# Mixture of experts streamed through one core: branch arms of 64 and 32 slots replaced by blocks of 32 slots with short conditionals

## The chip, the cores and the metric

One core of a Trainium2 chip runs the whole program. The metric is device time in microseconds for one execution, given as the median of several runs.

## The reference

The program computes one layer of a streaming encoder over 256 tokens of width 1024: a normalised input goes through three branches (sparse attention, a convolution, attention into a memory), which are gated, summed and projected; after a layer norm comes a mixture of experts, which is where the change lies. Each token takes its 4 best of 32 experts:

```python
logits = (xt @ w_router + b_router)
top_v, top_e = lax.top_k(logits, 4)
gate = softmax(top_v)
# for each expert e, over the tokens that chose it:
hdn = xb @ w1[e] + b1[e]                 # 1024 -> 2048
g, u = split(hdn, 2)
g = minimum(g, 7.0); u = clip(u, -7.0, 7.0)
y = ((u + 1.0) * (g * sigmoid(1.702 * g))) @ w2[e] + b2[e]   # 1024 -> 1024
out = segment_sum(y * gate, token)
h = layer_norm(alpha * h + out)
```

No token is dropped, so an expert has as many rows as tokens chose it. With these inputs the counts, from e0 to e31, are 60, 0, 26, 3, 27, 68, 3, 42, 94, 26, 85, 5, 48, 40, 24, 62, 34, 43, 9, 17, 23, 32, 18, 12, 8, 140, 3, 36, 13, 15, 3, 5. The counts are known on the chip only, at run time. All weights are fp32, 12 MB for an expert.

## The kernel before

The first 298 us or so of the span are the attention, convolution and memory branches, the router and its top 4. They are the same in both kernels. What follows is a loop over 32 experts, unrolled in the program.

**Weights.** Each expert's weights are 12 blocks of 1 MB: eight row blocks of w1, four of w2. The queue of the sync engine (SP) issues all 384 in order (`send`, L107 and L109) into a ring of buffers; 20 blocks are in flight or in use at once. A DMA waits until the block that held its buffer is given back by TensorE (PE).

**One expert.** `onehot` and `gather` pick the tokens' rows by matmuls with a 0/1 matrix `dd` into PSUM tile PX; `turn` transposes them into `xT`, one expert ahead. `gate_up` adds the bias by a matmul (L1085) and multiplies by w1 row block by row block (L1088); `act` is the clamped SwiGLU on VectorE (DVE) and ScalarE (ACT); `turn` transposes its result (L1052), `down` multiplies by w2 (L1108 for the bias, L1115) into PY. `places` (L1120, L1121) makes the matrix that brings an expert's rows back to their tokens, `scatter` (L1135) adds the rows, split in a high and a low part by `split_y` (L1128, L1129), to four PSUM banks PO, an expert later. PO starts as alpha times h1 (L1191).

**Forms.** For up to 32 tokens 32 slots are used, four quarters of the columns side by side in one bank; for more, 64 slots in two banks, PG and PU, with twice the time of PE for the same weights. PE, ACT and DVE load the count of an expert into a register and choose between two arms, `If(n > 32)` / `Else` (L1232). The 64 arm holds behind its expert another conditional for more than 64 tokens (L1234), whose body `more` handles the next 64 slots, again in two forms (L1166), and nests itself (L1176).

**Order of the work.** The program text sets it on each engine. A block is given back to the ring by a semaphore of PE. Inside an arm the instructions of PE count for that semaphore in each arm alike only at the end of the arms, so an SP wait on a block used in an arm stands at the join. A mark ahead of `down` (L1200) tells PE's sequencer where the next expert's branch will go.

## Time and profile before

| what | value |
|---|---|
| median of 3 runs | 1406.69 us (1404.11 to 1408.3) |
| profiled execution | 1408.23 us, span 1406.5 us |
| mean granted clock of PE | 0.896 |
| PE busy | 1105.9 us, 79% of the span |
| weight and other DMA by the main queue | 449.2 MB, 80.2% of 16 engines' span |

The profile shows one execution. Times are microseconds from the span's start. "Idle before, released by" at a row is the time for which the engine did nothing just ahead of it and what ended that; "issue" means that nothing the profile shows was waited for. Branches are recorded apart from the busy time, as the sequencer's own (PEldq, DVEq, ACTq).

### The profile page before, as it was taken

Reading aid. Unit: us, or ns where it says so; the run is one execution under the profiler, and the core shown is the slowest. Engines: PE = TensorE matmul, PEld = TensorE weight load, DVE = VectorE, ACT = ScalarE, POOL = GpSimd, SP = SyncE. Lnnn points to the kernel's source line nnn. Section 1 sums busy time; section 2 is a strip of 40 time slices with the busy share of each in tenths; the row PEclk is TensorE's granted clock in tenths of the full one; section 3 lists DMA queues with packets and bytes.
Section 4 is the critical chain, followed back from the end, with each engine's and each line's share of the span. In section 5 each row is a group of like instructions: output and inputs, shape, how many; then the busy total and the mean of one; then the engine's idle time right before and its main releaser. Section 6 shows DMA issues by size and latency. Waiting matters only on the chain. (4 is left out here: it accounts for less than half of the span.)

```text
span 1406.5 us, 16745 instructions
## 1 busy us (share of the span) xinstructions
PE 1105.9 (79%) x6722; PEld 507.6 (36%) x6722; DVE 440.8 (31%) x957; ACT 276.9 (20%) x522; POOL 98.3 (7%) x107
## 2 busy tenths in 40 slices
PE   8899989977878867859677698867767788596774
PEld 8788779822312222313222232222112122132211
DVE  7897997741111211202111111111111111121113
ACT  6458865530100100101000000000000000010000
POOL 2307640010000000000000000000000000000001
PEclk9999999998889988979988899989787899898977
DMA  8553277755999789749399999899999993399994
GB/s 294 188 195 121 91 277 250 263 191 238 413 414 416 318 344 414 322 171 416 136 403 413 396 416 411 358 376 413 415 413 415 414 416 133 130 417 413 412 414 195
DMA packets 85829, 451.65 MB, mean 321 GB/s; under 512 B 8016, under 2 KB 8144, under 8 KB 52784
## 3 DMA queue, kind: packets, MB, share of 16 engines
q1 hardware_dynamic: 85648, 449.20, 80.2%
q8 instruction: 118, 1.93, 0.6%
q14 instruction: 63, 0.52, 0.1%
HBM read 448.12 MB, written 1.05 MB: 319 GB/s over the span
## 5 line engine op out<-in xcount | busy, mean ns | idle before, releaser
L1088 PE MATMUL PG<-w,RES 128*32 128x512 f32 (+1 forms) x1952 | 357.1, 721 | 65.8 <-DMA w<-in_w_dram 51.3
L1115 PE MATMUL PY<-w,aa 128*32 128x512 f32 (+1 forms) x1184 | 196.2, 604 | 9.6 <-DMA w<-in_w_dram 9.5
L1088 PEld LDWEIGHTS PG<-w,RES 128*32 128x32 f32 (+1 forms) x1952 | 82.1, 129 | 281.4 <-issue 164.5
L1097 ACT ACTIVATE aa<-RES 128x256 f32<-128x256 f32 (+1 forms) x37 | 18.3, 494 | 668.9 <-DVE RES L1096 668.9
L1085 PE MATMUL PG<-BB,sel 96*32 96x512 bf16 (+1 forms) x122 | 19.7, 479 | 140.7 <-issue 126.4
L1088 PE MATMUL PU<-w,RES 128*64 128x512 f32 x416 | 110.9, 612 | 0.0
L267 PE MATMUL mm<-hh,whi 128*128 128x256 f32 x352 | 102.0, 290 | 11.1 <-DVE hh L366 6.1
L1122 DVE TENSOR_SCALAR sc<-PY,SXE 128x256 fp32r<-128x256 f32 x32 | 15.5, 484 | 292.8 <-PE PY L1121 292.8
L1115 PEld LDWEIGHTS PY<-w,aa 128*32 128x32 f32 (+1 forms) x1184 | 63.5, 120 | 112.4 <-issue 71.5
L269 PE MATMUL mm<-hh,wlo 128*128 128x256 f32 x352 | 98.7, 280 | 0.2 <-DVE wlo L221 0.2
L268 PE MATMUL mm<-hl,whi 128*128 128x256 f32 x352 | 98.8, 281 | 0.0
L1096 DVE TENSOR_SCALAR RES<-PG 128x256 f32<-128x256 f32 (+1 forms) x37 | 19.2, 518 | 253.5 <-PE PG L1088 253.5
L221 DVE TENSOR_TENSOR wlo<-raw,whi 128x1024 fp32r<-128x1024 f32 (+1 forms) x74 | 92.1, 1253 | 9.6 <-ACT whi L213 5.8
L1129 DVE SCALAR_TENSOR_TENSOR yy<-PY,gs,yy 128x512 fp32r<-128x512 f32 x32 | 24.0, 750 | 192.1 <-ACT yy L1128 132.5
L213 ACT ACTIVATE whi<-raw 128x1024 fp32r<-128x1024 f32 (+1 forms) x74 | 76.1, 1030 | 14.6 <-DMA raw<-in_wf_dram 13.4
L141 POOL TENSOR_TENSOR l20r<-l20a,mhalf 128x1 f32<-128x1 f32 x1 | 0.6, 570 | 1100.6 <-DVE l20a L139 1100.6
L267 PEld LDWEIGHTS mm<-hh,whi 128*128 128x128 f32 x352 | 66.6, 189 | 15.3 <-DVE hh L366 6.3
L667 POOL TENSOR_TENSOR cv<-cv,ct 128x256 f32<-128x256 f32 x70 | 63.8, 912 | 57.1 <-ACT ct L666 52.5
L269 PEld LDWEIGHTS mm<-hh,wlo 128*128 128x128 f32 x352 | 66.7, 189 | 0.4 <-DVE wlo L221 0.4
L268 PEld LDWEIGHTS mm<-hl,whi 128*128 128x128 f32 x352 | 66.5, 189 | 0.4 <-DVE hl L367 0.2
L1085 PEld LDWEIGHTS <-sel 96*32 96x32 bf16 (+1 forms) x148 | 6.7, 104 | 165.3 <-issue 164.6
L1044 PE MATMUL PX<-h,dd 128*64 128x512 f32 x256 | 63.5, 617 | 0.0
(323 smaller groups left out, 1233.9 us busy)
## 6 DMA issues: line engine op xcount, KB each, us to landing
w<-in_w_dram SPq DMA_DIRECT2D x384, 1024.0 KB, 20.1
raw<-in_wf_dram SPq DMA_DIRECT2D x70, 512.0 KB, 3.7
rb<-in_rows_dram SPq DMA_DIRECT2D x3, 512.0 KB, 6.2
mT<-in_memt_dram SPq DMA_DIRECT2D x4, 256.0 KB, 5.5
raw<-in_wf_dram SPq DMA_DIRECT2D x4, 256.0 KB, 5.3
xt<-in_x_dram SPq DMA_DIRECT2D x2, 512.0 KB, 5.5
rw<-in_rows_dram SPq DMA_DIRECT2D x2, 512.0 KB, 4.8
r<-in_rows_dram SPq DMA_DIRECT2D x2, 512.0 KB, 17.4
```

What stands on the lines that cost most here:

```text
L213: S.activation(parts[i][:, c], raw[i][:, c], AF.Copy)
L221: V.tensor_tensor(lo[:, c], raw[i][:, c], parts[i][:, c].bitcast(F32), op=OP.subtract)
L267: PE.matmul(o, lhsT=wh, rhs=xh, start=first, stop=False)
L268: PE.matmul(o, lhsT=wh, rhs=xl, start=False, stop=False)
L269: PE.matmul(o, lhsT=wl, rhs=xh, start=False, stop=last)
L667: G.tensor_tensor(o, o, ct, op=OP.add)
L1044: PE.matmul(PX[q * 64:q * 64 + 64, :], lhsT=dd[:, t, :].bitcast(F32), rhs=h1[:, t, q * 512:q * 512 + 512], start=t == 0, stop=t == 1)
L1085: PE.matmul(o, lhsT=one_of, rhs=BB1[:, p, c], start=True, stop=False)
L1088: PE.matmul(o, lhsT=xs(k), rhs=WT[e, 1, k][:, p, c], start=False, stop=k == KD - 1)
L1096: V.tensor_scalar(g[:, :w], pg, 7.0, None, op0=OP.min)
L1115: PE.matmul(PY[r:r + m, :], lhsT=xs(k), rhs=WT[e, 2, k // 2][:, k % 2, q * 512:q * 512 + 512], start=i == 0 and h > 0, stop=i == len(ks) - 1)
L1129: V.scalar_tensor_tensor(yl, PY, gs, yh.bitcast(F32), op0=OP.mult, op1=OP.subtract)
```

## The change

Every block of slots is now 32 wide, and the two arms are gone.

- `first(e, xs, o, ks)` adds two row blocks of w1 for one block of 32 slots into a bank; `second` half of w2. Block 1 uses banks PG and PY, block 2 PU and PU, block 3 PY and PG.
- `past(n, f)` calls f for block 2 inside `If(n > 32)` and, nested, for block 3 inside `If(n > 64)`. It stands behind every pair of row blocks of w1 (four times an expert) and behind each half of w2 (twice).
- Whatever block 2 and 3 need besides stands in conditionals of its own: `act`, `turn_a`, `split_y`, `scatter`, and in `enter` their slots and, for block 3, a gather of their own.
- More than 96 tokens: `further` runs blocks 4 and up ahead of the expert, a body of some 1240 instructions of PE that is jumped over otherwise. The mark that names a jump's target now names the jump over this body.
- `enter(e + 1)` makes the scatter matrix at the end of the expert before, rather than beside the expert's own matmuls; the h1 matmuls into PO stand ahead of expert 0 rather than in it.

```diff
+    def past(n, f, b=1):
+        if b < 3:
+            with tc.If(n > 32 * b):
+                f(b)
+                past(n, f, b + 1)
...
+    def enter(e, n):
+        places(e)
+        slots(0, scs[e % 2], gc)
+        with tc.If(n > 32):
+            slots(1, s2s[e % 2], g2)
+            with tc.If(n > 64):
+                onehot(e, 64, dd)
+                gather(dd)
+                turn_x(x2)
+
+    def expert(e, prev, n, nxt):
+        with tc.If(n > 96, label=f"p{e}"):
+            further(e, n, 3)
+        if nxt is not None:
             onehot(e + 1, 0, dd)
-        gate_up(e, lambda k: kcol(xT, 64)(k)[:, :m], m, beside)
-        if e:
+        banks = (PG, PU, PY)
+        xs = [xcol(xT, 0), xcol(xT, 1), xcol(x2, 0)]
+        for k in range(0, KD, 2):
+            first(e, xs[0], PG, (k, k + 1))
+            past(n, lambda b: first(e, xs[b], banks[b], (k, k + 1)))
+        if prev is not None:
             scatter(scs[(e - 1) % 2], ys)
+            with tc.If(prev > 32):
+                scatter(s2s[(e - 1) % 2], y2)
+        act(PG, ab[:, 0, :])
+        with tc.If(n > 32):
+            act(PU, ab[:, 1, :])
...
+        if nxt is not None:
+            tc.mark_branch_hint_location(f"p{e + 1}", hint=(nxt > 96), engines=[ET.PE])
+        outs = (PY, PU, PG)
+        for i2 in range(2):
+            second(e, aT[0], PY, i2)
+            past(n, lambda b: second(e, aT[b], outs[b], i2))
+        split_y(PY, gc, ys)
+        with tc.If(n > 32):
+            split_y(PU, g2, y2)
+            with tc.If(n > 64):
+                scatter(s2s[e % 2], y2)
+                places(e)
+                slots(2, s2s[e % 2], g2)
+                split_y(PG, g2, y2)
+        if nxt is not None:
+            enter(e + 1, nxt)
...
     for e in range(NE):
         while sent[0] < 12 * e + 12:
             send()
-        n = counts.pop(e)
-        count(e + 1)
-        with tc.If(n > 32, label=f"x{e}") as c:
-            expert(e, 64)
-            with tc.If(n > 64):
-                more(e, n, 64)
-        with c.Else():
-            expert(e, 32)
+        counts[2] = count(e + 1)
+        expert(e, *counts)
+        counts = counts[1:] + [None]
```

On PE, in the 32 arm of expert 0 before, the row blocks of w1 (each w with a number of its own) follow each other, with only the two matmuls of `places` between them:

```order
L1085 MATMUL PG_3502<-BB1_2280,sel_75 32x512
L1088 MATMUL PG_3502<-w_588,RES_81 32x512 x4
L1088 MATMUL PG_3502<-w_711,RES_81 32x512 x4
L1088 MATMUL PG_3502<-w_878,RES_81 32x512 x4
L1120 LDWEIGHTS idb_74
L1120 MATMUL PY_3505<-posT_3520,idb_74 128x256
L1121 MATMUL PY_3505<-tl_3387,ident_63 128x256
L1088 MATMUL PG_3502<-w_1053,RES_81 32x512 x4
L1088 MATMUL PG_3502<-w_2327,RES_81 32x512 x4
L1088 MATMUL PG_3502<-w_2372,RES_81 32x512 x4
```

After, at the same place, blocks 2 (PU) and 3 (PY) of a pair stand behind that pair, each behind a branch that PE takes when the block has no tokens:

```order
L1078 MATMUL PG_3499<-w_875,RES_78 32x512 x4
L1078 MATMUL PG_3499<-w_1050,RES_78 32x512 x4
L1065 COMPARE_AND_BRANCH
L1078 MATMUL PU_3500<-w_875,RES_78 32x512 x4
L1078 MATMUL PU_3500<-w_1050,RES_78 32x512 x4
L1065 COMPARE_AND_BRANCH
L1078 MATMUL PY_3502<-w_875,RES_78 32x512 x4
L1078 MATMUL PY_3502<-w_1050,RES_78 32x512 x4
L1065 UNCONDITIONAL_BRANCH x3
L1078 MATMUL PG_3499<-w_2324,RES_78 32x512 x4
```

Two branches now stand between one pair and the next, where none stood; the matmuls on a pair are the same for block 1.

On SP, before, at the first blocks behind the ring's first filling (the names are buffers of w1 and w2), two branches mark the places where an expert's conditionals end, and several DMAs between them wait for a DMA queue alone:

```order
L1232 UNCONDITIONAL_BRANCH
L109 DMA w_4271<-in_w2_dram 128x2x1024 [waits DMAHW3_49,PE_49]
L109 DMA w_4273<-in_w2_dram 128x2x1024 [waits DMAHW4_49,PE_49]
L109 DMA w_4275<-in_w2_dram 128x2x1024 [waits DMAHW5_49]
L109 DMA w_4277<-in_w2_dram 128x2x1024 [waits DMAHW6_49]
L107 DMA w_4958<-in_w1_dram 128x2048 [waits DMAHW7_49]
L1232 UNCONDITIONAL_BRANCH
L107 DMA w_4960<-in_w1_dram 128x2048 [waits DMAHW0_49]
```

After, each of these DMAs waits for PE, and one or two stand behind the branch of each pair:

```order
L1183 UNCONDITIONAL_BRANCH
L1065 UNCONDITIONAL_BRANCH
L109 DMA w_4298<-in_w2_dram 128x2x1024 [waits DMAHW3_49,PE_49]
L1065 UNCONDITIONAL_BRANCH
L109 DMA w_4300<-in_w2_dram 128x2x1024 [waits DMAHW4_49,PE_49]
L1065 UNCONDITIONAL_BRANCH x2
L109 DMA w_4302<-in_w2_dram 128x2x1024 [waits DMAHW5_49,PE_49]
L1197 UNCONDITIONAL_BRANCH
L109 DMA w_4304<-in_w2_dram 128x2x1024 [waits DMAHW6_49,PE_49]
L1204 UNCONDITIONAL_BRANCH
L107 DMA w_5001<-in_w1_dram 128x2048 [waits DMAHW7_49,PE_49]
```

The DMAs moved from behind one join of an expert to places behind its single conditionals.

## Rows read from the trace of the kernel before

**Rows 1.** Waits of SP's DMA queue: us in total, times, longest us.

```profile
SPq L109 <- PEq L1176: 164.2, 4, 58.1
SPq L109 <- PEq L1234: 124.4, 8, 33.8
```

**Rows 2.** Windows: us, busy of PE, PEld, DVE, ACT, POOL, clock, DMA share, GB/s.

```profile
440.00:956.00 516.00, 397.90 (x2177) 134.41 (x2179) 89.89 (x233) 42.54 (x86) 0.00 (x0) 0.89 0.87 353
956.00:1128.00 172.00, 127.55 (x764) 35.27 (x765) 25.68 (x76) 12.86 (x30) 0.00 (x0) 0.84 1.02 414
```

**Rows 3.** Timeline of small expert e26: start, us, engine line, operation, idle before.

```profile
1227.00 0.65 PE L1085 MATMUL PG<-BB,sel 96*32 96x512 bf16 x4 [11.86 <-issue]
1227.38 4.36 PE L1088 MATMUL PG<-w,RES 128*32 128x512 f32 x24
...
1231.68 0.28 PE L1120 MATMUL PY<-posT,idb 32*128 32x256 bf16 x1
1231.80 0.59 PE L1121 MATMUL PY<-tl,ident 32*128 32x256 f32 x2
...
1232.32 4.50 PE L1088 MATMUL PG<-w,RES 128*32 128x512 f32 x40
...
1236.75 1.20 PE L1135 MATMUL PO<-yy,sc 64*128 64x512 f32 x8
...
1237.88 1.94 PE L1044 MATMUL PX<-h,dd 128*64 128x512 f32 x8
...
1244.86 0.41 PE L1085 MATMUL PG<-BB,sel 96*64 96x512 bf16 x2
```

**Rows 4.** Timeline of PE in medium expert e7, and e8's first rows.

```profile
524.00 0.41 PE L1085 MATMUL PG<-BB,sel 96*64 96x512 bf16 x2
...
543.68 7.03 PE L1115 MATMUL PY<-w,aa 128*64 128x512 f32 x32
558.88 0.64 PE L1085 MATMUL PG<-BB,sel 96*64 96x512 bf16 x2 [8.17 <-issue]
```

**Rows 5.** Timeline at the end of large expert e8 and start of e9.

```profile
615.93 3.01 SPq L109 DMA_DIRECT2D w<-in_w_dram  x4
...
625.69 0.65 PE L1085 MATMUL PG<-BB,sel 96*32 96x512 bf16 x4 [12.54 <-issue]
...
631.28 0.27 PEld L1088 LDWEIGHTS PG<-w,RES 128*32 128x32 f32 x7 [3.27 <-issue]
```

**Rows 6.** Branch lines: engine, operation, count, ns min/median/max, first to last start.

```profile
L1232 PEldq COMPARE_BRANCH  x32: 78/2452/6118, 298.6 to 1356.3; - x32
L1232 DVEq COMPARE_BRANCH  x32: 50/56/63, 302.1 to 1359.0; - x32
...
L1234 PEldq COMPARE_BRANCH  x20: 83/4686/6233, 325.2 to 1273.5; - x20
...
L1234 PEldq EVENT_SEMAPHORE  x8: 51/51/51, 329.7 to 1273.4; - x8
...
L1166 PEldq COMPARE_BRANCH  x6: 73/340/359, 477.2 to 1198.4; - x6
```

**Rows 7.** The down matmuls' line: same columns.

```profile
L1115 PE MATMUL PY<-w,aa x1184: 589/592/1063, 322.6 to 1389.8; 128*32 128x512 f32 x128, 128*64 128x512 f32 x70
```

**Rows 8.** Timeline of e25: its first row, and its last block of 32 slots.

```profile
1127.87 0.41 PE L1085 MATMUL PG<-BB,sel 96*64 96x512 bf16 x2
...
1199.22 7.04 PE L1088 MATMUL PG<-w,RES 128*32 128x512 f32 x64
...
1206.37 0.42 DVE L1096 TENSOR_SCALAR RES<-PG 128x256 f32<-128x256 f32 x1 [5.33 <-PE PG L1088]
...
1208.95 3.64 PE L1115 MATMUL PY<-w,aa 128*32 128x512 f32 x32
```

**Rows 9.** Timeline at the loop's first matmuls and behind the last down matmul.

```profile
298.79 0.64 PE L1085 MATMUL PG<-BB,sel 96*64 96x512 bf16 x2 [1.22 <-DVE tl L1034]
...
315.52 3.70 PE L1191 MATMUL PO<-h,al 128*128 128x512 f32 x8
...
1390.88 0.69 ACT L1128 ACTIVATE yy<-PY,gs 128x512 fp32r<-128x512 f32 x1 [9.87 <-PE PY L1115]
```

## The prediction, written before the changed kernel ran

> **What bounds the kernel now.** I read the waits of the DMA queue first, because the change is about when weight blocks come free. Two rows stand out: the weight DMAs stood 164.2 us behind the join of L1176 and 124.4 us behind that of L1234 [rows 1]. These are joins of experts with more than 32 tokens, where a block is given back only when the whole conditional is over. Then I read the table of windows: from 440 to 956 us, where the medium and large experts lie, the weights came at 353 GB/s; from 956 to 1128 us, where nearly all are small, at 414 GB/s with the DMA engines full [rows 2]. One block of 1 MB (1.049 MB) at 414 GB/s is 2.53 us, twelve of an expert 30.4 us. So the program alternates: TensorE (PE) paces experts over 32 tokens, DMA the rest. Last I read what PE does in one expert of each kind, which the terms below need. The trace has 20 small experts (up to 32 tokens), 8 medium (to 64), 3 large (to 96) and one of 140, e25.

> **DMA after the change.** With returns pair by pair the waits behind joins shrink or go. 364 blocks behind the first 20 take 364 x 2.53 = 921 us; started near 313 us (the first pair's end, below) they would land by 1234 us. The last down matmul of before ended at 1390.9, when the scaling behind it started [rows 9]. If only DMA counted, that is some 150 us of gain. So what is late next is PE's own row of instructions, and I price it expert by expert.

> **A skip.** Behind each of the four pairs of w1 and the two halves of w2, PE meets a conditional for block 2. For a small expert it jumps over it. No row of before shows this jump over a short body in the midst of matmuls. The nearest are the jump over a 64 arm of a later block, L1166, median 340 ns, and the 51 ns of PE's semaphore instruction at a join, L1234 [rows 6]. The path also brings PE's own count up to date, which waits until earlier matmuls are done: a matmul lasts 592 ns [rows 7], while a group of four is issued every 0.43 us (40 in 4.50 us [rows 3]: (4.50 - 0.59)/9). So 0.16 us of a group still hangs over when the next would start. Estimate: 0.34 + 0.05 + 0.16 = 0.55 us. Lower end 0.05 (a compare that costs DVE 56 ns [rows 6] and nothing drained), upper end 0.34 + 0.59 = 0.93 us (a whole matmul and the branch). I take 0.55, the sum of the nearest rows. A small expert passes ten of them (six pairs, and those for scatter, transposes, end and entry), and one with nothing in flight, 0.39.

> **The far jump.** The body for more than 96 tokens now stands ahead of every expert and all but e25 jump over it: one far jump per expert, as before's jump into the small arm. Rows: L1232 took 78 ns at least, 2452 in the median, 6118 at most, L1234 4686 in the median [rows 6]. The hint that names the target stays ahead of the down matmuls, so I take 2.45. e0 has no hint behind it; there I take 5.3, between the median of L1234 and the maximum. Behind a far jump the stream of instructions can run dry: in e9 the weight loads stood 3.27 us on issue between two groups of the same loop, 5.6 us behind the expert's first matmul [rows 5]. A small expert's path is now stretched over more instructions (three blocks of which one runs), so this comes oftener; I take half of 3.27, 1.6 us, for each small, bounds 0 and 3.27.

> **Small, s.** e26 ran from 1227.00 to the next expert's 1244.86 [rows 3]: 17.9 us; its first 24 matmuls took 4.36 us, while 40 later ones took 4.50, so it began at the lower of the two clock levels: 24 warm ones are 6 groups, 5 x 0.43 + 0.59 = 2.74 us, 1.6 less. That is 16.2 warm. After: 16.2 + 10 x 0.55 + 0.39 + 1.6 + 2.45 = 26.2 us.

> **Medium, m.** e7 ran from 524.00 to the end of its down matmuls at 543.68 + 7.03 = 550.7, 26.7 us, then 8.17 us of nothing [rows 4]. The matmul work of two 32 blocks is the same (7.04 + 3.64 us for a block [rows 8], against a 64 block's 7.03 for down alone). New: the second block's chain from L1096 to the down matmuls, of which 1.7 us is not beside the first's (bounds 0 and the whole 2.6, 1206.37 to 1208.95 [rows 8]); its scatter, 1.20 us for eight matmuls [rows 3], in three of eight cases on the path, 0.4; six jumps over block 3, each 0.55 + 0.34 for the nested second jump, 5.3; three other skips, 1.65; the far jump, 2.45. m = 26.7 + 1.7 + 0.4 + 5.3 + 1.65 + 2.45 = 38.2.

> **Large, l, and e25.** Three blocks of 7.04 + 3.64 [rows 8] are 32.0; biases of 0.8 each 2.4; two scatters 2.4; places (0.28 + 0.59) twice 1.7; gathers of 1.94 [rows 3] twice 3.9; three act chains of 2.6 [rows 8] 7.8; some 3.4 for transposes and copies, an estimate; no skips but the jump, 2.45: 56 us, where e8 took from 558.88 to 625.69 [rows 4, 5], 66.8. There the refill that sits inside the join is late too: SP issued only at 615.93 and PE stood 12.54 us [rows 5]. e25 took 99.1 (1127.87 to 1227.00 [rows 3, 8]); after: 56 plus two more blocks of 18.6 (10.7 of matmuls, 7.9 of chain, bias, places and scatter) plus 4.4 of gather and turn, 98.

> **Sum.** e0's first bias matmul stood at 298.79 [rows 9]. Ahead of it come now the eight h1 matmuls, 3.70 [rows 9] (they stood beside the loop and are in e0's price no more), places 0.9, a skip 0.55 and the unhinted jump 5.3: 309. Then 20 x 26.2 + 8 x 38.2 + 3 x 56 + 98 = 524 + 305.6 + 168 + 98 = 1095.6. The last expert has no jump and no entry of a next one, -3. From the last down matmul to the span's end are 1406.5 - 1390.9 = 15.6, and the profiled execution was 1.7 above its span (1408.23). 309 + 1095.6 - 3 + 15.6 + 1.7 = 1419 in the terms of the profiled execution, which is 1.5 above the median of the runs: 1418 us. DMA stays ahead of this: seven smalls in a row, e18 to e24, take 183 us on PE, their 84 blocks less the 20 in the ring 162.

> So the gain behind the joins is spent on skips: 200 of the small and 72 of the medium experts at 0.55 are 150 us, of the order of what DMA alone would give back.

> **Rivals.**
> (a) Faster. A skip costs the branch alone, 0.30, and pages are there in time, so no 1.6. s = 16.2 + 3 + 0.4 + 2.45 = 22.1, m = 35.7, l = 53, e25 95: sum 442 + 286 + 159 + 95 = 982, end 1305. But then smalls in a row run into DMA at 30.4 us each as from 956 to 1128 us now [rows 2]: e18 to e24 would take 7 us more than PE alone with a full ring at their start (162 against 155), 58 with an empty one (7 x 8.3); I take the middle, 33, so 1340. For it: the gaps of 8 and 12 us behind the joins [rows 4, 5] are real and go. Against it: PE's median far and near branches take 6 to 84 times DVE's 56 ns [rows 6].
> (b) No change: the skip is 0.51 instead of 0.55, and the sum falls by 272 x 0.04 = 11 us to 1407. This is the point of balance: below 0.51 the change wins, above it loses.
> (c) Much slower: every far jump is paid in full, 6.1 instead of 2.45, because the jumps inside an expert make PE lose what it had fetched for the hinted target, and the dry stand of 3.27 comes each time. 31 x 3.65 + 20 x 1.65 = 146 us more: 1564. For it: L1234's median 4686 with 6233 at most [rows 6], where a hint stood but other code ran in between. [...]
> (d) That the change doesn't return blocks early: no row speaks for it, since in the new order each weight DMA waits for PE behind its own pair; 0.02, priced as (c).

> **How the numbers follow.** The likeliest case is the sum, 1418, chance 0.45, with its own range of 1395 to 1475: the chain of a second block, and a skip between 0.47 and 0.75. Rival (a) 0.33, (b) 0.07, (c) and (d) 0.15. The whole range goes from 1335, the middle of (a), to 1510: a skip of 0.93 alone would give 1418 + 272 x 0.38 = 1521, all of (c) is left out above, and the lower half of (a), where a skip of 0.05 would leave only the DMA, at 1234 + 17 = 1251 and more. A measurement of this kernel tells 0.3%, about 4 us, from no change. Faster by more: (a) and the lower edge of the sum, 0.39. Within: 0.08. Slower: 0.53.

> **What would show it.** Right: no SP wait on a join of tens of us; small experts some 26 us apart with PE standing about 0.5 us on issue behind each pair; mediums near 38, larges near 56; the far jump at its old median. Wrong: pairs of matmuls that follow each other without a stand (then (a)), waits of PE on weights in most smalls (DMA is the bound, (a)), or a stand of 5 us and more at the head of every expert (c).

## The result and the profile after

The changed kernel takes 1460.74 us (median of 4 runs, 1455.21 to 1461.73) against 1407.49 before: ratio 1.0363, 95% interval 1.0314 to 1.0412. It is slower, as forecast, and by 53 us rather than the 11 that the prediction gave: 1460.7 against 1418, inside the range of 1335 to 1510. The span of the profiled execution is 1459.0 us.

The return of weights does what the change says. These are the waits of SP's DMA queue after, with the columns of [rows 1]:

```profile
SPq L109 <- PEq L1065: 293.3, 53, 15.9
SPq L107 <- PEq L1065: 280.1, 84, 10.1
SPq L109 <- PE PY L1078: 118.2, 16, 56.4
```

The long single waits of 58.1 and 33.8 us of [rows 1] are gone from the joins; SP now waits often and for at most 15.9 us behind the pairs. One long wait is left, the 56.4 us of the third row: it lies in e25, whose far body uses all blocks of the expert before its pairs give back the first. That SP's total is larger says nothing bad: SP is early. What counts is whether PE waits for weights. Here are the main groups of PE's matmuls in the expert loop of the changed kernel (line, tile, count, busy and mean ns, then idle time ahead of them and what ended it):

```profile
L1078 PE MATMUL PG<-w,RES 128*32 128x512 f32 x2048 | 303.6, 718 | 27.4 <-PEq L1065 26.4 <-DMA w<-in_w_dram 1.0
L1075 PE MATMUL PG<-BB,sel 96*32 96x512 bf16 x136 | 20.3, 585 | 113.4 <-PEq L1183 67.6 <-DVEq L1183 37.0 <-issue 3.9
L1100 PE MATMUL PY<-BB,sel 96*32 96x512 bf16 x64 | 13.1, 401 | 19.0 <-DVEq L1204 13.1 <-DVEq L1206 5.5 <-issue 0.2
L1113 PE MATMUL PX<-posT,idb 32*128 32x256 bf16 x38 | 10.7, 280 | 50.2 <-DVEq L1216 31.2 <-DVEq L1218 13.2 <-DVE RES L1119 4.2
```

Before, the same view had these groups, the first with the longest waits for weights, the other two the heads of the experts in the two arms:

```profile
L1088 PE MATMUL PG<-w,RES 128*32 128x512 f32 x1536 | 242.7, 746 | 58.2 <-DMA w<-in_w_dram 43.6 <-issue 14.4
L1085 PE MATMUL PG<-BB,sel 96*32 96x512 bf16 x96 | 13.2, 476 | 111.5 <-issue 98.4 <-DVE dd L1039 11.1 <-DVE yy L1129 2.0
L1085 PE MATMUL PG<-BB,sel 96*64 96x512 bf16 x26 | 6.4, 490 | 29.2 <-issue 28.0 <-DVE tl L1034 1.2
```

The wait for weights falls from 43.6 to 1.0 us in this group, and from 61 to 1 over all groups of the loop. The heads of the experts (L1085, now L1075) stood 140.7 us in the two arms together and stand 113.4 now, named by the far jump's conditional, L1183. And new waits stand where none were: PE waits for DVE's passage of a conditional, 37.0 at L1183, 31.2 and 13.2 at L1216 and L1218, 13.1 and 5.5 at L1204 and L1206: 100 us together. The stands at the pairs, PEq L1065, come to some 42 us with those of the other groups (138 of 0.30 us). From 298.5 us to the end of the last product PE's idle time is 254 us before and 281 after; its busy time is 838 and 864. The two differences, 26 each, make the loss.

The experts share it unevenly. From an expert's first bias matmul to the next expert's, the three larges together fall from 198.0 to 152.3 us and the eight mediums rise from 296.6 to 316.2. Eighteen of the smalls (all but e24, behind which e25's far body runs, and e31, the last) rise from 435.1 to 508.2. The change pays in the larges and costs more than that in the experts that skip.

One small expert's end shows the new wait. This is the timeline of e6's last rows and e7's first:

```profile
530.63 1.50 PE L1108 MATMUL PY<-w,aa 128*32 128x512 f32 x12
532.18 0.69 ACT L1124 ACTIVATE yy<-PY,gc 128x512 fp32r<-128x512 f32 x1 [3.97 <-PE PY L1108]
532.90 0.75 DVE L1125 SCALAR_TENSOR_TENSOR yy<-PY,gc,yy 128x512 fp32r<-128x512 f32 x1 [5.11 <-ACTq L1216]
533.77 0.28 PE L1113 MATMUL PX<-posT,idb 32*128 32x256 bf16 x1 [1.64 <-DVEq L1216]
533.89 0.59 PE L1114 MATMUL PX<-tl,ident 32*128 32x256 f32 x2
534.52 0.48 DVE L1118 TENSOR_SCALAR sc<-PX,sx 128x256 fp32r<-128x256 f32 x1 [0.87 <-PE PX L1114]
535.98 0.42 DVE L1119 SCALAR_TENSOR_TENSOR RES<-s,PX 128x256 f32<-128x256 f32 x1
537.39 0.62 PE L1075 MATMUL PG<-BB,sel 96*32 96x512 bf16 x4 [2.91 <-DVEq L1183]
537.50 0.42 DVE L1029 TENSOR_SCALAR dd<-i,pos 128x64 fp32r<-128x64 bf16 x2 [1.10 <-DVEq L1183]
```

The last product ends at 532.13. PE's place matmuls of `enter` need PX, and a skipped body (the third block's end) would have let DVE read PX; so PE waits until DVE, which is still scaling the result, has passed that conditional (1.64 us). The next bias writes PG, and the skipped far body would have let DVE read PG; so PE waits until DVE has made the slots and passed L1183 (2.91 us). 5.3 us lie between two experts. Before, the first bias behind e26 followed without idle time [rows 3], though other heads stood up to 13.4 us.

Where the jump is long, it hides the second wait. The branch lines after (columns of [rows 6]):

```profile
L1183 PEldq COMPARE_BRANCH  x32: 73/1098/5106, 305.5 to 1422.1; - x32
...
L1065 PEldq COMPARE_BRANCH  x336: 65/207/4987, 312.0 to 1441.4; - x168
```

The far jump's median is 1098 ns against the 2452 of [rows 6], but it runs from 3.6 to 5.1 us for nearly all experts from e18 on; and in e1 to e4 and e6, where it is short, the first skip behind it takes 2.8 to 5.0. These are the branch's own records: PE's matmuls stand less at such a skip, 1.9 us at most, since the first pair is still running. Of the twenty smalls eleven have the long jump, five the long first skip and e9, e11 and e14 neither; e31's jump takes 2.8.

### The profile page after: what moved, and what is told of

It is laid out like the page before. It is cut to its first block, busy times and chain, and to the rows that moved or that the text cites. A ratio compares the mean times of both kernels' runs of the same rounds, so it can differ in the third digit from the quotient of the medians.

```text
span 1459.0 us, 22186 instructions
## 1 busy us (share of the span) xinstructions
PE 1136.3 (78%) x8155; PEld 524.2 (36%) x8155; DVE 464.3 (32%) x1070; ACT 291.4 (20%) x561; POOL 97.8 (7%) x105
## 5 line engine op out<-in xcount | busy, mean ns | idle before, releaser
L1078 PE MATMUL PG<-w,RES 128*32 128x512 f32 x2048 | 303.6, 718 | 27.4 <-PEq L1065 26.4
L1078 PEld LDWEIGHTS PG<-w,RES 128*32 128x32 f32 x2048 | 70.9, 125 | 231.9 <-issue 224.6
L1083 ACT ACTIVATE RES<-RES 128x256 f32<-128x256 f32 x50 | 20.9, 417 | 624.8 <-DVE RES L1082 624.7
L1108 PE MATMUL PY<-w,aa 128*32 128x512 f32 x1024 | 136.7, 620 | 7.6 <-PEq L1065 7.6
L1075 PE MATMUL PG<-BB,sel 96*32 96x512 bf16 x136 | 20.3, 585 | 113.4 <-PEq L1183 67.6
L218 DVE TENSOR_TENSOR wlo<-raw,whi 128x1024 fp32r<-128x1024 f32 (+1 forms) x74 | 92.0, 1251 | 12.4 <-ACT whi L210 6.7
L1035 PE MATMUL PX<-h,dd 128*64 128x512 f32 x296 | 80.1, 667 | 20.1 <-DVE dd L1029 10.3
L1078 PE MATMUL PU<-w,RES 128*32 128x512 f32 x768 | 95.0, 613 | 0.0
L1125 DVE SCALAR_TENSOR_TENSOR yy<-PY,gc,yy 128x512 fp32r<-128x512 f32 x32 | 24.0, 750 | 201.3 <-ACTq L1216 102.6
L264 PEld LDWEIGHTS mm<-hh,whi 128*128 128x128 f32 x352 | 68.2, 194 | 15.6 <-DVE hh L363 6.5
L1108 PEld LDWEIGHTS PY<-w,aa 128*32 128x32 f32 x1024 | 42.1, 112 | 68.4 <-issue 53.5
L1108 PE MATMUL PU<-w,aa 128*32 128x512 f32 x448 | 62.3, 614 | 0.1
L1075 PEld LDWEIGHTS <-sel 96*32 96x32 bf16 x200 | 6.9, 111 | 137.0 <-issue 89.3
```

The costliest lines, as they stand in the source:

```text
L218: V.tensor_tensor(lo[:, c], raw[i][:, c], parts[i][:, c].bitcast(F32), op=OP.subtract)
L264: PE.matmul(o, lhsT=wh, rhs=xh, start=first, stop=False)
L1035: PE.matmul(PX[q * 64:q * 64 + 64, :], lhsT=dd[:, t, :].bitcast(F32), rhs=h1[:, t, q * 512:q * 512 + 512], start=t == 0, stop=t == 1)
L1075: PE.matmul(y, lhsT=sel[:, e:e + 1].to_broadcast([96, 32]), rhs=BB1[:, :, c], start=True, stop=False)
L1078: PE.matmul(y, lhsT=xs(k), rhs=WT[e, 1, k][:, :, c], start=False, stop=k == KD - 1)
L1083: S.activation(s, g, AF.Sigmoid, scale=1.702)
```

## The experiments

Three theories were set against each other. J (joins): PE stands because a skipped conditional makes it wait for DVE's passage. F (fetch): the code that the far jump over the body for more than 96 tokens goes to, and the code behind it, arrive late; the prediction and the expectations call such code a page. P (pair skips): the conditionals behind every pair cost. A fourth, W, holds that the return by pairs is worth something by itself. Ratios are to the kernel before on the same chip; the changed kernel stands at 1.0363.

**Entry early.** `enter(e + 1)` between the halves of w2.

```diff
             past(n, lambda b: second(e, aT[b], outs[b], i2))
+            if i2 == 0 and nxt is not None:
+                enter(e + 1, nxt)
...
-        if nxt is not None:
-            enter(e + 1, nxt)
```

> The entry of the next expert (its two place matmuls and the slots on VectorE) stands between the two halves of w2 instead of behind the scaling of the result; the two scale columns are doubled for it. Theory J (joins): TensorE stands at the end of every expert because VectorE's part of a skipped conditional has to be passed first, 44 us at L1216 and L1218 and 37 us at L1183. With the entry early the first wait goes and the second shrinks, about 2.5 us an expert: 1375 to 1400 us. Theory F (fetch): the end of an expert is set by the far jump's page, which comes when it comes: 1445 to 1460 us. Theory P (pair skips): no pair skip is touched, 1455 to 1460 us.

Measured 1428.96 us, ratio 1.0106 (1.0051 to 1.0160): some 36 us better against before's runs beside it. The waits, in the view used above:

```profile
L1075 PE MATMUL PG<-BB,sel 96*32 96x512 bf16 x136 | 17.7, 509 | 131.0 <-PEq L1184 93.2 <-DVEq L1184 32.5 <-issue 5.1
...
L1113 PE MATMUL PX<-posT,idb 32*128 32x256 bf16 x38 | 10.4, 273 | 8.9 <-PEq L1065 7.3 <-DVE tl L1023 1.5
```

The 44.4 us at L1216 and L1218 went. But the jump's own stand (now L1184) grew from 67.6 to 93.2: read with theory F, PE reaches it sooner and its code is not there yet. Neither theory's number holds; J names the wait, F takes part of the gain back. In the loop PE's idle time falls by 21 us and its busy time by 15; the mean granted clock of the profiled execution is 0.919 against 0.892.

**The far body in another bank.** PG becomes PY in `further`.

```diff
-            first(e, xcol(x3, j), PG, range(KD))
-            act(PG, aT[3])
-            turn_a(aT[3], PG[:, 0:256], aT[0])
+            first(e, xcol(x3, j), PY, range(KD))
+            act(PY, aT[3])
+            turn_a(aT[3], PY[:, 0:256], aT[0])
```

> The body for more than 96 tokens, which all experts but e25 jump over, uses bank PY in place of PG; the work is the same. Theory J: the first bias matmul writes PG and waits at L1183 for VectorE only because the skipped body reads PG; the 37 us on VectorE at L1183 go in the experts whose jump is short, 1420 to 1435 us. Theory F and theory P: no change, 1455 to 1465 us.

Measured 1432.18, ratio 1.0147 (1.0083 to 1.0210).

```profile
L1075 PE MATMUL PG<-BB,sel 96*32 96x512 bf16 x128 | 17.7, 537 | 88.8 <-PEq L1183 76.4 <-issue 5.5 <-DVEq L1177 4.2
```

The 37.0 us of waiting for DVE at L1183 are gone without any work moved: only the bank that a skipped body names has changed. That is theory J's mechanism, shown, and the time lies in J's range. The jump's stand rises by 9, those at L1078 behind the pairs from 26.4 to 35.1. In the loop idle time falls by 16 us only, busy time by 15, at a mean granted clock of 0.912. How much of these 15 is the clock was not tested apart.

**No far body.** The conditional for more than 96 tokens and its mark are left out, and with them 44 of e25's 140 tokens.

```diff
-        with tc.If(n > 96, label=f"p{e}"):
-            further(e, n, 3)
```

> Leaves out the body for more than 96 tokens with its conditional and its hint, so the last 44 tokens of e25 are not computed: about 54 us less by that alone (e25's two further blocks), 1406. Theory F: the jump's 67.6 us and the page stands at the first pair (some 30 us) go as well: 1310 us. Theory J: of the 107.8 us at L1183 the jump part goes, the wait for VectorE at the entry's join stays for 2 us an expert: 1335 us. Theory P: 1400 us.

Measured 1299.21, ratio 0.9193 (0.9142 to 0.9243). Of the 161 us against the changed kernel some 54 are the work left out (from e24's first bias to e25's took 82.1 us there, of other small experts' 28). The other 107 go with the conditional, busy time at a higher mean granted clock (0.942 against 0.892) among them. F came nearest. A small expert falls from a median of 28.2 us to 23.3, a medium from 38.8 to 35.6.

```profile
L1075 PE MATMUL PG<-BB,sel 96*32 96x512 bf16 x128 | 15.7, 436 | 18.2 <-DVE sc L1118 14.4 <-DVE y__3520 L1125 3.6
```

The stand at the head of an expert is 18.2 us instead of 113.4. The far conditional is the largest single cost, twice all that the change lost; before had a far jump too, so this is not by itself the difference.

**A shorter far body.** Blocks 4 and 5 alone.

```diff
                 block(1)
-                with tc.If(n > 32 * b + 64):
-                    further(e, n, b + 2)
```

> The body for more than 96 tokens holds blocks 4 and 5 only and does not nest further (enough for 160 tokens); same work here, but the jump over it is far shorter. Theory F: if the price of the jump is its length, the 4.8 us jumps of e18 to e31 and the page stands of 4.7 us shrink: 1400 to 1430 us. Theory J: the waits for VectorE stay, 1440 to 1460 us. If a far jump costs the same whatever its length, 1455 to 1465.

Measured 1438.50, ratio 1.0162 (1.0102 to 1.0223). Between the theories, and other experts pay: the heads that stand for the jump are now e1 to e4 (4.2 to 5.9 us) and those from e26 on (2.0 to 6.0), and e18 to e22 stand 0.8 to 1.2 us at the first skip, behind a head that waited 2.1 us for DVE.

**Conditionals once a phase.**

```diff
-        for k in range(0, KD, 2):
-            first(e, xs[0], PG, (k, k + 1))
-            past(n, lambda b: first(e, xs[b], banks[b], (k, k + 1)))
+        first(e, xs[0], PG, range(KD))
+        past(n, lambda b: first(e, xs[b], banks[b], range(KD)))
```

and the same for `second`.

> Blocks 2 and 3 stand in one conditional behind all eight row blocks of w1 and one behind all of w2, instead of behind every pair: 2 of these skips an expert instead of 6. Theory P: a skip stands 0.30 us (41.7 us in 139 in the changed kernel), four of six go in 20 small and, nested, in 8 medium experts: 25 to 30 us less, 1430 to 1438. Theory W (the return of weight blocks pair by pair is worth something by itself): mediums and larges give their blocks back later, PE waits for weights again, no gain or a loss: 1455 to 1480. Theory F: 1445 to 1460.

Measured 1420.56, ratio 1.0050 (1.0023 to 1.0077): 44 us less by the ratios (0.0313 of 1410), more than P's 30. Waits for weights stay at 0.6 us:

```profile
L1078 PE MATMUL PG<-w,RES 128*32 128x512 f32 x2048 | 290.8, 720 | 11.5 <-issue 10.9 <-DMA w<-in_w_dram 0.6
```

W falls: giving blocks back at the end of a phase is enough, and giving them back by pairs costs more than it brings. The pairs cost more than their stands: in the loop idle time falls by 25 us and busy time by 16. The row shows 12.8 of the latter (303.6 to 290.8 us for the same 2048 matmuls): with a conditional behind it a pair's last matmul has ended before the next pair begins (0.17 to 0.19 us before, at the pairs of e6 in the changed kernel).

**Entry early, other bank and short far body together.** The three edits above.

> The entry early, the far body in bank PY, and the far body cut to blocks 4 and 5, together. Alone they gave 32, 28 and 22 us. Theory J: the first two take different waits (L1216 and L1183) and add up, 1390 to 1405 us, with no wait for VectorE left at the far jump. Theory F: what the joins gave back the jump takes, since a far jump is paid at the jump or at the first short branch behind it: 1415 to 1430 us, with the same long stands of PE's sequencer.

Measured 1414.96, ratio 1.0023 (0.9998 to 1.0048), at the lower edge of what F expected. PE's waits for DVE at L1182 and at the entry are gone, but the jump's stand is 96.7 us, and the edits that gave 36, 30 and 28 us alone give 48 together:

```profile
L1075 PE MATMUL PG<-BB,sel 96*32 96x512 bf16 x128 | 16.4, 498 | 109.1 <-PEq L1182 96.7 <-DVE y__3520 L1125 10.5 <-ACTq L1182 1.7
```

**These three, and conditionals once a phase.**

> The kernel with the three edits of the run before, and the conditionals of blocks 2 and 3 once a phase. Theory P: 25 to 30 us below that run. Theory W: not below it.

Measured 1400.68, ratio 0.9929 (0.9905 to 0.9953): 0.7% below before. The step from the run above is 13 us (0.0094 of 1410), where P expected 25 to 30 and W none; the jump's stand grows again:

```profile
L1075 PE MATMUL PG<-BB,sel 96*32 96x512 bf16 x128 | 17.8, 541 | 148.1 <-PEq L1182 135.8 <-DVE y__3520 L1125 7.9 <-DVEq L1182 2.6
```

**No mark.**

```diff
-            tc.mark_branch_hint_location(f"p{e + 1}", hint=(nxt > 96), engines=[ET.PE])
```

> The changed kernel without the mark that names the far jump's target. Theory F: the target's page is asked for only at the jump, so each of 31 jumps costs 5 to 6 us on PE's path instead of 0.1 to 5: 1500 to 1540 us. If the mark does nothing (the many branches between it and the jump undo it), 1455 to 1465 us. Theory J: as the first, less what the wait for VectorE hides (1.5 us of each): 1480 us.

Measured 1562.48, ratio 1.1086 (1.1047 to 1.1125). The jump:

```profile
L1183 PEldq COMPARE_BRANCH  x32: 73/6007/7044, 301.1 to 1515.9; - x32
```

An unmarked far jump takes 6.0 us in the median, and the mark was worth 102 us. The prediction's rival (c) priced the jumps in full at 31 x 3.65 = 113 us more. That its time of 1564 is met so closely is luck: it stands on the sum of 1418, which was 43 too low, and on dry stands besides. The changed kernel keeps most of the mark.

**The far body as one block of 64 slots.** Some 280 instructions are jumped over instead of 1240; entry early; no mark. In `further` the two blocks of 32 become one, with gate in PY, up in PU and the product in PG:

```diff
+        for k in range(KD):
+            for o, p, c in tiles:
+                PE.matmul(o, lhsT=col(x3, k), rhs=WT[e, 1, k][:, p, c], start=False, stop=k == KD - 1)
```

> Entry early, and the body for more than 96 tokens is one block of 64 slots (enough for 160 tokens) in place of two or more of 32: some 280 instructions of PE are jumped over, against 1240 in the changed kernel and some 500 in the run with a short far body; no mark for the jump. [...] Theory J: a jump is a jump, and without its mark it costs 3 us more, as the run without the mark showed: 1480 to 1520 us. Theory P: 1415.

Measured 1422.86, ratio 1.0076 (1.0047 to 1.0105): 57 us below J's range. If the price of a jump were its length, as F had it for the shorter far body, most of the stand at it would be gone. It is 100.9 us, against 96.7 in the run with early entry, other bank and short body:

```profile
L1077 PE MATMUL PG<-BB,sel 96*32 96x512 bf16 x128 | 16.8, 512 | 124.3 <-PEq L1202 100.9 <-issue 7.8 <-DVE y__3522 L1127 5.3
...
L1202 PEldq COMPARE_BRANCH  x33: 70/1552/6073, 302.0 to 1380.1; - x33
```

The median is far from the 6007 of the unmarked long jump, so a short distance seems to help (the early entry differs too), but jumps of up to 6.1 us and stands of up to 4.2 us at the first skip remain. The short body did not make the jump cheap.

**The same, conditionals once a phase.**

> The same with the conditionals of blocks 2 and 3 once a phase. Theory F: the 136 us of stands at the jump of the comparable run (1400.7 us) mostly go: 1275 to 1300 us. Theory W: with the jump gone DMA is nearer to being the bound, and the later return of blocks costs more than the skips: not below the run before. Theory J: 1470 to 1500 us.

Measured 1390.78, ratio 0.9850 (0.9783 to 0.9916): the fastest complete version, 1.5% below before, good for up to 160 tokens an expert. Against the run above the ratio falls by 0.0226, some 32 us, where W expected no gain. The stand at its jump is still 111.4 us, so F's 1275 to 1300 was missed:

```profile
L1077 PE MATMUL PG<-BB,sel 96*32 96x512 bf16 x128 | 16.4, 498 | 123.7 <-PEq L1202 111.4 <-DVE y__3522 L1127 5.3 <-DVEq L1202 5.3
```

**No weight stream.** The changed kernel with the first 20 blocks alone loaded.

```diff
+            if sent[0] >= RING:
+                WT[e, p, c] = keep[stream.index((e, p, c)) % RING]
+                sent[0] += 1
+                continue
```

> The changed kernel with the first 20 weight blocks alone loaded; all later experts multiply by these same buffers, so the weights of the experts behind are wrong and 364 MB are not moved. If PE's own chain sets the time and the weights wait for it (theories F, J and P alike), 1450 to 1465 us. If the weight stream slows the fetch of instructions, the long jumps fall from 4.8 us towards the 3.5 of e0, where no weights move: 1400 to 1430 us. If waits for weights that the profile does not show were part of it, below 1380.

Measured 1423.78, ratio 1.0087 (1.0064 to 1.0111). The branch lines of the jump and of the pairs:

```profile
L1189 PEldq COMPARE_BRANCH  x32: 73/961/3392, 304.6 to 1388.4; - x32
...
L1071 PEldq COMPARE_BRANCH  x336: 65/202/2627, 310.5 to 1406.6; - x168
```

With 364 blocks not moved the kernel is only 39 us faster by the ratios, so weights hardly set the changed kernel's time. The time lies in the range given for a stream that slows the fetch. PE's stands at the heads of e18 to e30 (without e25) fall to between 3.0 and 3.7 us from 4.3 to 6.1, the longest jump falls to 3392 ns from 5106, and the longest skip behind a pair to 2627 from 4987. Waits for DVE are the same to 0.2 us (37.0 at the jump, 31.2 and 13.2 at the entry). So jumps and the first skips behind them take longer beside the weight stream. What it does to the time comes mostly that way: PE's stands at the jump fall from 67.6 to 42.8 us and those at L1084 (L1078 in the changed kernel) from 26.4 to 21.5, 30 of the 39.

**The 64 slot body, once a phase, with the mark.**

> The run e11 (entry early, far body one block of 64 slots, conditionals of blocks 2 and 3 once a phase) with the mark for the jump put back ahead of the second product. Theory F as it stands after these runs (a jump to code that is not yet fetched costs 5 to 6 us unless the mark has brought it, whatever the distance; with the mark some experts pay at the jump, some at the first skip behind it, some not): the mark gave 102 us to the changed kernel; here, where half of the unmarked jumps are short already, some 20 to 50 us: 1340 to 1370. [...]

Measured 1400.18, ratio 0.9914 (0.9886 to 0.9942): not the 1340 to 1370 of F. With the short body no gain from the mark is seen; its median jump is 3287 ns against 1662 without. Why was not shown.

## Why the prediction was right in sign and short in size

**The bound.** That PE's own row of instructions would set the time, not DMA, was right: 1.0 us of waits for weights, and with no stream behind the first 20 blocks still 1423.78. The sign was a narrow call, though, at 0.53 for slower and 0.39 for faster.

**The sum, by experts.** Predicted to the last product: 1401.6; measured 1443.3, 42 us more. Sixteen ordinary small experts took 27.6 us on average against 26.2 (+22). The two small and one medium experts ahead of a large one took 6 to 9 us more than predicted, since the large one's gather stands in their end, and the three larges 50.8 instead of 56: +6 together. Other mediums 38.7 against 38.2: +4. e25 with its far body +12, the start +3, the last expert -5.

**The term that was short: matmuls taken as warm.** In the sixteen smalls PE stood idle 8.3 us on average and was busy 19.2. The prediction's terms for standing come to the same 8.3: ten skips at 0.39 (0.55 less the 0.16 of matmul that hangs over), 0.39, 1.6 and 2.45. Its busy time was 16.2 and ten times 0.16, 17.8. So all of the 1.4 us that a small was short lie in busy time. The 16.2 came from e26 less 1.6 us for its start at the lower clock level (in the trace of before a granted clock of 0.50 from 1227.1 to 1230.4 us and of 1.00 from 1232.4 to 1236.9), and no reason was given why the other experts should start warm, at 1.00. They did not. These are the four pairs of e18, behind a stand of 4.79 us at its head:

```profile
964.74 3.65 PE L1078 MATMUL PG<-w,RES 128*32 128x512 f32 x16
968.57 2.56 PE L1078 MATMUL PG<-w,RES 128*32 128x512 f32 x16 [0.18 <-PEq L1065]
971.31 1.92 PE L1078 MATMUL PG<-w,RES 128*32 128x512 f32 x16 [0.18 <-PEq L1065]
973.40 1.92 PE L1078 MATMUL PG<-w,RES 128*32 128x512 f32 x16 [0.17 <-PEq L1065]
```

The granted clock is 0.50 from 964.36 to 968.50 and 1.00 from 970 to 980, the lower and the upper of the two levels in this trace. In all sixteen the first pair takes 2.8 to 3.7 us; first and second together cost 1.9 us an expert more than at 1.92 each. A row of before had shown it: from 956 to 1128 us, six smalls, PE was busy 127.55 us at a granted clock of 0.84 [rows 2], 21 us an expert.

**The cause that was missed: a skip waits for DVE.** The prediction let a skip wait for PE's own matmuls. At the pairs a stand is 0.30 us, near its 0.39. At the other conditionals PE waited for DVE, 0.65 us at L1204 (13.1 in 20), 1.64 at L1216 (31.2 in 19), 2.6 at L1183 where the jump was short (37.0 in 14). The run with the far body in another bank takes the last of these away by itself, and the early entry the second. That the stands agree in sum all the same is luck: these waits stand where ten equal skips and a dry stand were priced.

**The far jump.** Right in the mean, wrong in form. 2.45 for the jump and 1.6 for the dry stand behind it were taken as two terms, 4.05 together; the heads of the sixteen smalls stood 4.15 us on average, 3.29 of it on the jump and 0.86 on DVE. A dry stand showed only in e1 to e4, 1.9 us at most. The run without weights shows why the price was open: with no stream PE's stands at the jump came to 42.8 us instead of 67.6. Without its mark the jump took 6.0 us in the median, and the mark was worth 102 us here; how the mark works is not shown.

**The rivals.** (a) failed: skips were cheap at the pairs, as it assumed, but what was saved there was spent at the joins, and it too took the matmuls as warm. (b), no change, failed: the kernel is 3.6% slower. (c) was the right picture of the jumps in the kernel without its mark (6007 ns in the median); with the mark much of the jump is hidden (1098 ns). The cause that (c) gives, fetched code lost to the jumps inside an expert, was the author's guess and is not shown. (d) failed: the waits for weights went.

**Open.** Which experts pay at the jump and which at the first skip was not settled. The runs with other code lengths moved the set; the distance jumped over does not decide alone, since 280 instructions cost up to 6.1 us. How the sum divides between DVE's joins and the jump depends on the order in which they end, as the combined runs show, so the single gains don't add up. No run held the clock while a wait went, so what a stand costs by the lower clock behind it is read from rows and not tested. The larges' 5 us less than predicted was not followed to a term; the 3.4 us for transposes and copies in their price stood on no row.

## What to carry to other kernels

In this kernel a conditional that is skipped still orders the engines: PE stood 100 us for DVE to pass conditionals, and 37.0 of them went when a skipped body named another bank. So put the rare body's tiles where nobody waits soon, and let the engine that comes late pass it before the other needs them. Check first whether finer return of buffers removes a wait of the engine that sets the end; here the waits for weights were gone with one conditional a phase, and four more an expert cost 44 us (13 and 32 in the two other kernels from which they were taken). Price an engine's work at the clock that it will have behind the stands you price (in e18 0.50 behind 4.79 us, and a first pair of 3.65 us instead of 1.92), not at the clock of a stretch that ran without them. Here the rare long body was paid by the passes that jump over it: 107 us went with its conditional. The stands at its jump were longer beside the weight stream, 67.6 us against 42.8 without it.
